# Sixteen of 22 channel tiles of the feed-forward's output half as seven products of quarters

## The chip, the cores and the metric

The kernel runs on one core of one Trainium2 chip. The metric is the device time of one execution in microseconds. Before the change it is 1206.3 us, the median of 3 runs (1205.36 to 1207.64).

## What is computed

Two layers of a hybrid encoder on 512 tokens of 1024 channels, in float32. Of each layer the change touches two parts, cut here to what matters:

```python
# attention: the indexer's scores choose the keys
score = sum over 4 index heads of relu(qi . ki) * wi        # 512 x 512, chunk-causal
keep the 128 highest of each row; softmax over the kept keys for 8 heads; times v
# feed-forward, D_FF = 2816 = 22 tiles of 128 channels
gate, up = split(x @ w_ffn_in)                              # 1024 -> 2 x 2816
ffn = (silu(gate) * up) @ w_ffn_out                         # 2816 -> 1024
x = layer_norm(ALPHA * x + ffn + ple)
```

## The kernel before

All matrix products are made of three matmuls each: both operands are split into a high part (a copy to float32r, on ScalarE) and a low part (the difference, on VectorE), and high x high, high x low and low x high are summed in PSUM. `split` (line 462) does this for a weight of up to 1024 columns: `A.copy(h, src)`, then `low(V, l, src, h)`. Its results go to a ring of four buffers for high parts (`wh`) and four for low parts (`wl`).

The feed-forward's input half is worked off by `ffn_in(j)` (line 1100), j = 0 to 10, 256 channels of gate and of up at a time. It uses seven products of quarters in place of eight. The sums of quarters of x are made once (`X1T.sums`), those of the weights per j: two by DMAs that add into a tile `tt` (`load_sums`, line 1085: two plain loads on SyncE's queue, then two accumulating ones on GpSimd's), two by VectorE. A product here is 24 matmuls of 256 columns into one PSUM bank. At the end the gated result is split into one tile `HT[j]` with 2 x 2 x 512 columns: high and low, two channel tiles, 512 tokens.

The output half is plain: `ffn_out(f0, f1, last)` (line 1168) multiplies channel tiles f0 to f1 of HT with `w_ffn_out`, for each of two column halves n and four token blocks b, three matmuls of 512 columns per channel tile. HT is the stationary operand, the split weight the moving one. Then VectorE adds each of the four banks to the rows X. The groups stand between the ffn_in:

```python
        for j in range(4):
            ffn_in(j)
        ffn_out(0, 6, False)
        for j in range(4, 7):
            ffn_in(j)
        ffn_out(6, 12, False)
        for j in range(7, 9):
            ffn_in(j)
        ffn_out(12, 16, False)
```

So one ffn_in lies between the last HT of a group and its ffn_out. After ffn_in(9) and ffn_in(10), `ffn_out(16, 22, True, ...)` ends the layer.

The order of the work is set by a planner in the file. Every engine call is recorded by `Recorder`, and `Order.issue` (line 160) sorts all calls into one list: each engine takes, among what its costs say can start within a small window, what the program has first. Buffers of a pool are given out in the order of the due times. Each engine then runs its own list strictly in order. As all calls are issued at one line, the profile's rows all say L276; they are told apart by the names of the tiles.

SBUF is divided by pools: `big` has 15 tiles of 2048 float32 per partition (x, HT, tt, quarters and much else), `page` 10 tiles of 512, five more pages `P` for scores and attention weights, three for masks, `raw` two tiles for weights as loaded. PSUM has four banks `acc`, three `ps`, one `po`.

Of the kernel before, what the change touches and what calls it, by code (L numbers as in the profile page):

```python
# [11 lines left out]
F32 = mybir.dt.float32  # L12
# [16 lines left out]
NB = 4  # L29
# [301 lines left out]
def body(ctx: ExitStack, tc: tile.TileContext, x, p, positions, w_in, w_o, ln1_g, ln1_b,  # L331
# [17 lines left out]
    def PP(dt, name):  # L349
        return page.tile([128, 512], dt, name=name, tag="P", bufs=5)  # L350

# [12 lines left out]
    def low(eng, dst, src, hi):  # L364
        eng.tensor_tensor(out=dst, in0=src, in1=f32(hi), op=OP.subtract)
# [113 lines left out]
    def wrows(w, r0, nkt, c0, c1):  # L479
        return w[r0:r0 + nkt * 128, c0:c1].rearrange("(k p) n -> p k n", p=128)  # L480
# [246 lines left out]
    for ly in range(DEPTH):  # L727
# [6 lines left out]
        wsc = small.tile([128, NB, 4], F32, name="wsc", bufs=2)  # L734
        sco = [None] * NB
# [363 lines left out]

        def ffn_in(j):  # L1100
# [52 lines left out]
            A.activation(g2, ba, AF.Silu)  # L1153
            ht = HT[j] = T(FR, "HT").rearrange("p (e f t) -> p e f t", e=2, f=2)
            for i, (g, u) in enumerate(((g1, s2), (g2, s5))):
                V.scalar_tensor_tensor(u, u, -1.0, g, op0=OP.mult, op1=OP.mult)
                v, ts = u.rearrange("p (f t) -> p f t", f=2), slice(i * 256, (i + 1) * 256)
                A.copy(ht[:, 0, :, ts], v)
                low(V, ht[:, 1, :, ts], v, ht[:, 0, :, ts])

# [25 lines left out]
        load_sums(0)  # L1186
        for j in range(4):
            ffn_in(j)
        ffn_out(0, 6, False)
        for j in range(4, 7):  # L1190
            ffn_in(j)
        ffn_out(6, 12, False)
        for j in range(7, 9):
            ffn_in(j)
        ffn_out(12, 16, False)
        for j in range(9, 11):
            ffn_in(j)
# [33 lines left out]
```

## Time and profile before

| | |
|---|---|
| median of 3 runs | 1206.3 us |
| profiled execution, its time | 1206.69 us |
| its span, first to last instruction | 1205.0 us |
| TensorE busy in the span | 1181.0 us |
| VectorE busy | 911.2 us |
| ScalarE busy | 594.1 us |
[...]

The span leaves out 1.7 us around the first and last instruction. Busy is the time in which at least one instruction of the engine ran. A recorded instruction is longer than the step from its start to the next start, for matmuls and on VectorE, as the next one starts before its end is written. The two layers take about 600 us each; the feed-forward of the first lies at 260 to 590 us.

### The profile page before, as it was taken

The numbers are of one execution on the slowest core, as the hardware profiler recorded it, in microseconds if no ns is written. First come the engines' busy times: TensorE is split into PE (matmuls) and PEld (weight loads), VectorE is DVE, ScalarE is ACT, GpSimd is POOL, SyncE is SP. The second block draws the span as 40 slices with busy tenths as digits, with TensorE's granted clock in tenths as the row PEclk, the third lists the DMA queues.
The fourth block names the chain that finished last, engine by engine and source line by source line (L and its number), as shares of the span: only waits on it lengthen the run. The fifth ranks groups of instructions, "written<-read, shape, count | busy, mean of one in ns | idle before, by whom it ended". The sixth has DMA issues, their size and how long they took to land. (4 is left out here: it accounts for less than half of the span.)

```text
span 1205.0 us, 18516 instructions
## 1 busy us (share of the span) xinstructions
PE 1181.0 (98%) x7326; PEld 1053.9 (87%) x7326; DVE 911.2 (76%) x1612; ACT 594.1 (49%) x978; POOL 154.4 (13%) x126
## 2 busy tenths in 40 slices
PE   8999999999999999999999999999999999999997
PEld 7877878789989998989888878778899899899995
DVE  6799998968755755757788999887777477566667
ACT  5545785545633533525345458934465245244340
POOL 0005312110100100000010261121010000000001
PEclk8999999999999999999999999999999999999999
DMA  7232143187871862743511321524685656648141
GB/s 219 71 98 78 36 88 140 36 192 206 183 199 60 188 198 70 208 108 98 192 53 36 121 73 36 140 70 159 150 197 144 173 125 173 175 106 209 53 141 70
DMA packets 124903, 152.76 MB, mean 127 GB/s; under 512 B 6544, under 2 KB 94608, under 8 KB 124816
## 3 DMA queue, kind: packets, MB, share of 16 engines
q1 hardware_dynamic: 101584, 128.51, 33.4%
q0 software_dynamic: 23232, 23.07, 12.5%
q8 instruction: 57, 0.93, 0.3%
q14 instruction: 30, 0.25, 0.1%
HBM read 149.47 MB, written 2.10 MB: 126 GB/s over the span
## 5 line engine op out<-in xcount | busy, mean ns | idle before, releaser
L276 DVE TENSOR_TENSOR wl<-raw,wh 128x1024 fp32r<-128x1024 f32 x178 | 217.3, 1223 | 126.6 <-ACT wh L276 125.7
L276 ACT CAST wh<-raw 128x1024 fp32r<-128x1024 f32 x194 | 203.4, 1050 | 211.1 <-PE acc L276 138.8
L276 PE MATMUL acc<-x1s,wh 128*128 128x256 f32 x1408 | 254.7, 283 | 2.3 <-ACT fg L276 2.3
L276 PEld LDWEIGHTS acc<-x1s,wh 128*128 128x128 f32 x1408 | 219.6, 192 | 2.7 <-ACT fg L276 2.7
L276 PE MATMUL acc<-wh,HT 128*128 128x512 f32 x704 | 218.5, 389 | 0.1
L276 PE MATMUL acc<-x1s,wl 128*128 128x256 f32 x704 | 199.2, 283 | 0.0
L276 PE MATMUL acc<-x1q,wh 128*128 128x256 f32 x1056 | 191.3, 283 | 0.0
L276 PEld LDWEIGHTS acc<-x1q,wh 128*128 128x128 f32 x1056 | 165.2, 192 | 0.6
L276 PEld LDWEIGHTS acc<-wh,HT 128*128 128x128 f32 x704 | 132.1, 188 | 27.6 <-issue 0.5
L276 PE MATMUL acc<-x1q,wl 128*128 128x256 f32 x528 | 149.4, 283 | 0.0
L276 DVE TENSOR_TENSOR wl<-tt,wh 128x1024 fp32r<-128x1024 f32 x66 | 80.8, 1224 | 76.3 <-ACT wh L276 76.2
L276 PE MATMUL acc<-wl,HT 128*128 128x512 f32 x352 | 137.1, 389 | 0.0
L276 PEld LDWEIGHTS acc<-x1s,wl 128*128 128x128 f32 x704 | 135.2, 192 | 0.0
L276 ACT CAST wh<-tt 128x1024 fp32r<-128x1024 f32 x66 | 69.3, 1050 | 130.4 <-PE acc L276 69.3
L276 POOL DMA_DIRECT2D tt<-in_w_ffn_in x44 | 56.4, 1303 | 527.8 <-DMA tt<-in_w_ffn_in 394.2
L276 PEld LDWEIGHTS acc<-x1q,wl 128*128 128x128 f32 x528 | 101.3, 192 | 0.0
L276 PE MATMUL acc<-wh,x1q 128*128 128x512 f32 x256 | 80.2, 392 | 1.4 <-DVE x1q L276 1.0
L276 PEld LDWEIGHTS acc<-wl,HT 128*128 128x128 f32 x352 | 66.1, 188 | 13.5
L276 PE MATMUL acc<-wl,xth 128*128 128x512 f32 x192 | 75.4, 395 | 1.5 <-DVE wl L276 1.5
L276 PE MATMUL acc<-wh,xtl 128*128 128x512 f32 x192 | 75.0, 393 | 0.0
L276 PE MATMUL acc<-wh,xth 128*128 128x512 f32 x192 | 74.9, 396 | 0.1
L276 ACT COPY fg<-acc 128x512 f32<-128x512 f32 x66 | 38.7, 586 | 65.0 <-PE acc L276 65.0
(214 smaller groups left out, 2024.6 us busy)
## 6 DMA issues: line engine op xcount, KB each, us to landing
raw<-in_w_ffn_in SPq DMA_DIRECT2D x22, 1024.0 KB, 5.3
tt<-in_w_ffn_in SPq DMA_DIRECT2D x44, 512.0 KB, 6.0
tt<-in_w_ffn_in POOLq DMA_DIRECT2D x44, 512.0 KB, 7.0
raw<-in_w_ffn_out SPq DMA_DIRECT2D x16, 1024.0 KB, 5.2
raw<-in_w_in SPq DMA_DIRECT2D x12, 1024.0 KB, 5.4
raw<-in_w_ffn_in SPq DMA_DIRECT2D x22, 512.0 KB, 3.6
raw<-in_w_ple_gate SPq DMA_DIRECT2D x8, 1024.0 KB, 5.1
raw<-in_w_ffn_out SPq DMA_DIRECT2D x12, 512.0 KB, 3.8
```

What stands on the lines that cost most here:

```text
L276: o.ins = o.fn(*o.a, **o.k)
```

## The change

In each layer the channel tiles 0 to 15 of the output half (j = 0 to 7) are multiplied by seven products of quarters as well, in groups of three, three and two j (six, six and four channel tiles). Tiles 16 to 21 stay as they were. HT of j below 8 takes two big tiles instead of one: `ha` holds the quarters h11, h12, h22, `hb` four sums of quarters (P1, S2, S3, S4), each split into high and low. Two of the seven weight operands, t1 and t3, are made by accumulating DMAs into two more big tiles per group (`load_out`, called inside the group's last ffn_in), two by VectorE. A product is, per j, two token blocks of three matmuls of 512 columns. After each product VectorE adds its two banks to X or takes them off.

To make room, the pools change: `big` 17 tiles, `page` 8. The scores and masks of a layer now share one big tile, and the attention weights P lie in a ring of four slots in another. The diff, cut:

```diff
-    big = ctx.enter_context(tc.tile_pool(name="big", bufs=15))
-    page = ctx.enter_context(tc.tile_pool(name="page", bufs=10))
+    big = ctx.enter_context(tc.tile_pool(name="big", bufs=17))
+    page = ctx.enter_context(tc.tile_pool(name="page", bufs=8))
...
-            sc = sco[b] = PP(F32, "sc")[:, :L]
+            if not scores:
+                scores.append(T(F32, "sc"))
+            sc = sco[b] = scores[0][:, (b - 1) * 512:(b - 1) * 512 + L]
...
-            m = mask[b] = page.tile([128, 512], BF, name="mask", tag="mask", bufs=3)[:, :(b + 1) * 128]
+            o = (0, 1536, 1664, 256)[b]
+            m = mask[b] = scores[0][:, o:o + (b + 1) * 64].bitcast(BF)
...
+            ring = T(F32, "P").rearrange("p (i n) -> p i n", i=4)
...
-                P = P_[b, h] = PP(F32, "P")[:, :L]
+                P = P_[b, h] = ring[:, (8 * b + h) % 4, :L]
...
+            if js:
+                out_sums.append(load_out(js))
             load_sums(j + 1)
...
+            ha, hb = HT[j] = [T(FR, "HT").rearrange("p (e q) -> p e q", e=2) for _ in range(2)]
...
+            parts(ha, 0, s2)
+            parts(ha, 512, h22)
+            ya, yb = page_(), page_()
+            p1, y2, y3, y4 = ya[:, 0:256], ya[:, 256:512], yb[:, 0:256], yb[:, 256:512]
+            V.tensor_tensor(out=p1, in0=h22, in1=h21, op=OP.subtract)
+            V.scalar_tensor_tensor(y2, p1, -1.0, h11, op0=OP.mult, op1=OP.subtract)
+            parts(hb, 0, ya)
+            V.tensor_tensor(out=y3, in0=h11, in1=h21, op=OP.subtract)
+            V.scalar_tensor_tensor(y4, y2, -1.0, h12, op0=OP.mult, op1=OP.subtract)
+            parts(hb, 512, yb)
...
+        def load_out(js):
...
+            for first in (q[0][0], q[1][1]):
+                t = T(F32, "tt")[:, :n * 512]
+                v = t.rearrange("p (j n) -> p j n", j=n)
+                SY.dma_start(v, first)
+                G.dma_start(v, q[0][1], accum_op=OP.add)
+                ts.append(t)
...
+        def ffn_seven(js, loaded):
...
+            def product(banks, src, which, first):
...
+                for j0 in range(0, n, 2):
+                    m = min(2, n - j0)
+                    hl.append(split(src[:, j0 * 512:(j0 + m) * 512].rearrange("p (j n) -> p j n", j=m),
+                                    [m, 512], V))
+                for i in range(2):
+                    for k, j in enumerate(js):
...
+                        for z, (a_, b_) in enumerate(((hs[0], wh), (hs[0], wl), (hs[1], wh))):
+                            PE.matmul(banks[i], a_, b_, start=first and k + z == 0,
+                                      stop=k == n - 1 and z == 2, skip_group_check=True)
...
+            product(ba, w11, A11, True)
+            into(ba, 0, 0, OP.add)
+            product(bb, w21, A12, True)
+            into(bb, 0, 0, OP.add)
+            bc = [PS() for _ in range(2)]
+            product(bc, t1, P1, True)
+            into(bc, 1, 1, OP.subtract)
+            w22 = fetch(q[1][1])
+            V.tensor_tensor(out=t1, in0=t1, in1=w22, op=OP.add)
+            product(ba, t1, S2, False)
+            into(ba, 0, 1, OP.subtract)
+            product(bc, w22, S4, False)
+            into(bc, 0, 1, OP.subtract)
+            product(ba, t3, S3, False)
+            into(ba, 1, 1, OP.subtract)
+            V.tensor_tensor(out=w21, in0=w21, in1=t1, op=OP.add)
+            product(ba, w21, A22, False)
+            into(ba, 1, 0, OP.add)
...
-        for j in range(4):
-            ffn_in(j)
-        ffn_out(0, 6, False)
...
+        for js in ([0, 1, 2], [3, 4, 5], [6, 7]):
+            for j in js:
+                ffn_in(j, js if j == js[-1] else None)
+            ffn_seven(js, out_sums.pop())
+        for j in range(8, 11):
+            ffn_in(j)
```

The change also moves instructions on the engines. In the lists below numbers at the names tell tiles of one name apart; X_76 and X_77 are the rows of x, acc and ps PSUM banks, wh and wl the split weights, fg pages of the gated result.

VectorE in the first layer, where the first group of the output half begins. Before (ffn_in(3) has just ended; HT_790 is its result, the group multiplies the three HT ahead of it):

```order
L276 SCALAR_TENSOR_TENSOR fg_775<-fg_775,fg_789 128x512
L276 TENSOR_TENSOR HT_790<-fg_778,HT_790 128x2x256
L276 TENSOR_TENSOR HT_790<-fg_775,HT_790 128x2x256
L276 TENSOR_TENSOR wl_805<-raw_803,wh_804 128x1024
L276 TENSOR_TENSOR wl_807<-raw_803,wh_806 128x1024
L276 TENSOR_TENSOR wl_814<-raw_812,wh_813 128x1024
L276 TENSOR_TENSOR X_76<-acc_796,X_76 128x512
L276 TENSOR_TENSOR X_76<-acc_797,X_76 128x512
L276 TENSOR_TENSOR X_77<-acc_798,X_77 128x512
L276 TENSOR_TENSOR X_77<-acc_799,X_77 128x512
```

The group's next splits stand ahead of the adds, and the newest HT is not used until the group after.

VectorE at the same place with the change (ffn_in(2) has just ended; fg_738 and fg_739 hold the sums of its result, HT_736 and HT_737 are its two tiles, tt_711 is t1, raw_745 is w21, raw_760 w22):

```order
L276 TENSOR_TENSOR wl_753<-raw_745,wh_752 128x512
L276 TENSOR_TENSOR wl_757<-tt_711,wh_756 128x1024
L276 TENSOR_TENSOR X_76<-acc_742,X_76 128x512
L276 TENSOR_TENSOR wl_759<-tt_711,wh_758 128x512
L276 TENSOR_TENSOR tt_711<-tt_711,raw_760 128x1536
L276 TENSOR_TENSOR X_76<-acc_743,X_76 128x512
L276 TENSOR_TENSOR raw_745<-raw_745,tt_711 128x1536
L276 TENSOR_TENSOR wl_762<-tt_711,wh_761 128x1024
L276 TENSOR_TENSOR wl_764<-tt_711,wh_763 128x512
L276 TENSOR_TENSOR wl_766<-raw_760,wh_765 128x1024
L276 TENSOR_TENSOR HT_737<-fg_738,HT_737 128x512
L276 TENSOR_TENSOR HT_737<-fg_739,HT_737 128x512
```

Where splits and four adds to X stood, there are now adds to X, splits and the two in-place sums of 1536 columns; the low parts of HT_737 come last, and both sums stand ahead of the low part wl_762. Ahead of this piece stand one gated half, two low parts of HT_736, the sums of quarters and two adds to X.

TensorE at the same place with the change, from the end of P1's matmuls for the first two j (HT_677 and HT_706; HT_737 belongs to the third):

```order
L276 MATMUL ps_755<-wl_757,HT_706 128x512
L276 MATMUL ps_755<-wh_756,HT_706 128x512
L276 MATMUL acc_740<-wh_761,HT_677 128x512
L276 MATMUL acc_741<-wh_761,HT_677 128x512
L276 MATMUL acc_740<-wl_762,HT_677 128x512
L276 MATMUL acc_740<-wh_761,HT_677 128x512
L276 MATMUL acc_740<-wh_761,HT_706 128x512
L276 MATMUL acc_740<-wl_762,HT_706 128x512
L276 MATMUL acc_740<-wh_761,HT_706 128x512
L276 MATMUL acc_741<-wl_762,HT_677 128x512
L276 MATMUL ps_754<-wh_758,HT_737 128x512
L276 MATMUL ps_754<-wl_759,HT_737 128x512
```

P1 is broken off after two of its three j, six matmuls of S2 on acc_740 and two on acc_741 are put in, and P1's matmuls for the third j follow. Before, the list runs the same HT through four banks in turn:

```order
L276 MATMUL acc_796<-wh_792,HT_712 128x512
L276 MATMUL acc_796<-wl_793,HT_712 128x512
L276 MATMUL acc_796<-wh_792,HT_712 128x512 x2
L276 MATMUL acc_796<-wl_793,HT_712 128x512
L276 MATMUL acc_796<-wh_792,HT_712 128x512
L276 MATMUL acc_797<-wh_792,HT_712 128x512
```

Up to the first group of the feed-forward's output half TensorE's list has the same instructions in the same order as before.

## Rows read from the trace of the kernel before

**Rows 1.** The page, part 1: busy us (share of span) x instructions.

```profile
PE 1181.0 (98%) x7326; PEld 1053.9 (87%) x7326; DVE 911.2 (76%) x1612; ACT 594.1 (49%) x978; POOL 154.4 (13%) x126
```

**Rows 2.** Busy time by 25 us stretch; columns in the first line.

```profile
core 0: us, PE busy (x) PEld busy (x) DVE busy (x) ACT busy (x) POOL busy (x), PEclk, DMA share, GB/s
75.00:100.00 25.00, 23.47 (x114) 19.36 (x113) 24.51 (x65) 10.63 (x16) 9.70 (x9) 1.00 0.37 127
100.00:125.00 25.00, 24.02 (x123) 19.77 (x122) 24.53 (x49) 13.01 (x23) 12.19 (x10) 1.00 0.16 50
300.00:325.00 25.00, 25.00 (x211) 25.00 (x210) 19.55 (x21) 13.79 (x18) 5.08 (x4) 1.00 0.73 177
350.00:375.00 25.00, 25.00 (x112) 20.70 (x111) 11.13 (x12) 4.62 (x5) 1.95 (x2) 1.00 0.47 105
```

**Rows 3.** Groups by line, VectorE and ScalarE, 250 to 590 us; page columns of part 5.

```profile
L276 DVE TENSOR_TENSOR wl<-raw,wh 128x1024 fp32r<-128x1024 f32 x65 | 79.5, 1223 | 57.6 <-ACT wh L276 57.5
L276 DVE TENSOR_TENSOR X<-acc,X 128x512 f32<-128x512 f32 x28 | 18.5, 686 | 7.2 <-PE acc L276 7.2
L276 DVE TENSOR_TENSOR HT<-fg,HT 128x512 fp32r<-128x512 f32 x22 | 14.6, 688 | 0.8
L276 DVE TENSOR_TENSOR tt<-tt,raw 128x1024 f32<-128x1024 f32 x11 | 13.5, 1225 | 0.9 <-DMA raw<-in_w_ffn_in 0.6
L276 DVE TENSOR_TENSOR wal<-raw,wah 128x256 fp32r<-128x256 f32 x2 | 0.9, 426 | 0.1
L276 ACT CAST wh<-raw 128x1024 fp32r<-128x1024 f32 x65 | 68.2, 1049 | 74.5 <-PE acc L276 60.5 <-DVE raw L276 8.6 <-issue 2.9
L276 ACT CAST HT<-fg 128x512 fp32r<-128x512 f32 x22 | 13.4, 619 | 1.8 <-DVE fg L276 1.8
```

**Rows 4.** Timeline of VectorE: start us, us, instruction, [idle before].

```profile
300.02 1.23 DVE L276 TENSOR_TENSOR tt<-tt,raw 128x1024 f32<-128x1024 f32 x1
301.16 0.68 DVE L276 TENSOR_TENSOR fg<-acc,fg 128x512 f32<-128x512 f32 x1
303.58 1.28 DVE L276 SCALAR_TENSOR_TENSOR fg<-fg 128x512 f32<-128x512 f32 x2
315.64 0.68 DVE L276 TENSOR_TENSOR fg<-acc,fg 128x512 f32<-128x512 f32 x1
316.24 1.22 DVE L276 TENSOR_TENSOR wl<-raw,wh 128x1024 fp32r<-128x1024 f32 x1
```

**Rows 5.** Timeline where the last ffn_in ahead of an ffn_out ends.

```profile
343.52 0.28 PE L276 MATMUL acc<-x1q,wl 128*128 128x256 f32 x1
343.64 0.40 PE L276 MATMUL acc<-wh,HT 128*128 128x512 f32 x1
343.84 0.60 ACT L276 ACTIVATE fg<-acc 128x512 f32<-128x512 f32 x1 [1.38 <-PE acc L276]
344.47 0.69 DVE L276 SCALAR_TENSOR_TENSOR fg<-fg 128x512 f32<-128x512 f32 x1 [0.68 <-ACT fg L276]
345.08 1.46 DVE L276 TENSOR_TENSOR HT<-fg,HT 128x512 fp32r<-128x512 f32 x2
```

**Rows 6.** Timeline of a wait of the matmuls for VectorE.

```profile
83.84 2.35 DVE L276 TENSOR_TENSOR wl<-raw,wh 128x1024 fp32r<-128x1024 f32 x2
85.11 0.50 PE L276 MATMUL acc<-wl,xth 128*128 128x512 f32 x1 [1.53 <-DVE wl L276]
85.45 0.40 PE L276 MATMUL acc<-wh,xtl 128*128 128x512 f32 x1
```

**Rows 7.** The page, part 6: DMA issues, KB each, us to landing.

```profile
tt<-in_w_ffn_in SPq DMA_DIRECT2D x44, 512.0 KB, 6.0
tt<-in_w_ffn_in POOLq DMA_DIRECT2D x44, 512.0 KB, 7.0
raw<-in_w_ffn_out SPq DMA_DIRECT2D x16, 1024.0 KB, 5.2
raw<-in_w_ffn_out SPq DMA_DIRECT2D x12, 512.0 KB, 3.8
```

More of the change, by code (lines that the diff above doesn't have):

```diff
@@ L347, in PG @@
         return page.tile([128, n], dt, name=name, tag="page")
-    def PP(dt, name):
-        return page.tile([128, 512], dt, name=name, tag="P", bufs=5)
     def ACC():
@@ L734, in body @@
         wsc = small.tile([128, NB, 4], F32, name="wsc", bufs=2)
-        sco = [None] * NB
+        sco, scores = [None] * NB, []
         mask = [mask0] + [None] * 3
@@ L1098, in load_sums, with ffn_in @@
                 G.dma_start(v[:, i], wrows(wf_l, 0, 4, DFF + c0, DFF + c0 + 256), accum_op=OP.add)
-        def ffn_in(j):
+        PLAIN = 8
+        out_sums = []
+        def ffn_in(j, js=None):
             c0 = j * 256
@@ L1153, in ffn_in @@
             A.activation(g2, ba, AF.Silu)
[L1154 to L1155 removed]
+            for u, g in ((s2, g1), (s5, g2)):
                 V.scalar_tensor_tensor(u, u, -1.0, g, op0=OP.mult, op1=OP.mult)
[L1157 to L1159 removed]
+            if j >= PLAIN:
+                ht = HT[j] = T(FR, "HT").rearrange("p (e f t) -> p e f t", e=2, f=2)
+                for i, u in enumerate((s2, s5)):
+                    v, ts = u.rearrange("p (f t) -> p f t", f=2), slice(i * 256, (i + 1) * 256)
+                    A.copy(ht[:, 0, :, ts], v)
+                    low(V, ht[:, 1, :, ts], v, ht[:, 0, :, ts])
+                return
@@ new lines, in ffn_in, with parts @@
+            ha, hb = HT[j] = [T(FR, "HT").rearrange("p (e q) -> p e q", e=2) for _ in range(2)]
+            def parts(t, q0, src):
+                q = slice(q0, q0 + src.free_size())
+                A.copy(t[:, 0, q], src)
+                low(V, t[:, 1, q], src, t[:, 0, q])
+            h11, h12, h21, h22 = s2[:, 0:256], s2[:, 256:512], s5[:, 0:256], s5[:, 256:512]
+            parts(ha, 0, s2)
+            parts(ha, 512, h22)
+            ya, yb = page_(), page_()
+            p1, y2, y3, y4 = ya[:, 0:256], ya[:, 256:512], yb[:, 0:256], yb[:, 256:512]
@@ new lines, in ffn_in @@
+            V.tensor_tensor(out=p1, in0=h22, in1=h21, op=OP.subtract)
[5 more added lines that the diff above has]
+        def load_out(js):
+            n = len(js)
+            w = wfo_l[js[0] * 256:(js[-1] + 1) * 256].rearrange("(j e p) n -> e p j n", e=2, p=128)
+            q = [[w[e][:, :, i * 512:(i + 1) * 512] for i in range(2)] for e in range(2)]
+            ts = []
+            for first in (q[0][0], q[1][1]):
[4 more added lines that the diff above has]
+                ts.append(t)
+            return q, ts
@@ new lines, in ffn_seven, with fetch, into @@
+        def ffn_seven(js, loaded):
+            n = len(js)
+            q, (t1, t3) = loaded
+            def fetch(src):
+                return raw(lambda t: [(t[:, :n * 512].rearrange("p (j n) -> p j n", j=n), src)])[:, :n * 512]
+            def product(banks, src, which, first):
+                hl = []
+                for j0 in range(0, n, 2):
[4 more added lines that the diff above has]
+                    for k, j in enumerate(js):
+                        wh, wl = (x[:, k % 2] for x in hl[k // 2])
+                        t = HT[j][which // 3 > 0]
+                        o = (which if which < 3 else which - 3) * 256 + i * 128
+                        hs = t[:, 0, o:o + 128], t[:, 1, o:o + 128]
+                        for z, (a_, b_) in enumerate(((hs[0], wh), (hs[0], wl), (hs[1], wh))):
+                            PE.matmul(banks[i], a_, b_, start=first and k + z == 0,
+                                      stop=k == n - 1 and z == 2, skip_group_check=True)
+            def into(banks, half, cols, op):
+                cs = slice(cols * 512, (cols + 1) * 512)
+                for i in range(2):
+                    x = Xb(2 * half + i)[:, cs]
+                    if op == OP.add:
+                        V.tensor_tensor(out=x, in0=banks[i], in1=x, op=op)
+                    else:
+                        V.tensor_tensor(out=x, in0=x, in1=banks[i], op=op)
+            A11, A12, A22, P1, S2, S3, S4 = range(7)
+            ba, bb = [ACC() for _ in range(2)], [ACC() for _ in range(2)]
+            w11, w21 = fetch(q[0][0]), fetch(q[1][0])
+            product(ba, w11, A11, True)
[16 more added lines that the diff above has]
+            into(ba, 1, 0, OP.add)
```

7 lines of the change are left out of this document (removed).

## The prediction

> **What bounds the kernel now.** The page's first part comes first: TensorE is busy for 1181.0 of 1205.0 us, VectorE for 911.2 [rows 1]. Busy times are averages, so the table of stretches comes next. In the feed-forward TensorE is busy for the whole 25 us of a stretch at a clock of 1.00, with an ffn_in (300 to 325) as with an ffn_out (350 to 375); VectorE has 19.55 and 11.13 us to do there [rows 2]. In attention (75 to 125) VectorE is nearly full with 24.5 us and TensorE idles for 1 to 1.5 us [rows 2]. So in the stage that is changed the time is TensorE's: a matmul that goes is worth its step, as long as the other engines hand over in time. They do so now; VectorE waits for casts there (57.6 us ahead of the weights' low parts) [rows 3].
>
> The step of a matmul is read from the counts, since records overlap. In the ffn_out stretch 112 matmuls of 512 columns fill 25 us: 0.223 us each. An ffn_in's are 211 in 25 us, 0.118 each [rows 2].
>
> **What goes from TensorE.** For channel tiles 0 to 15 the plain form takes 16 tiles x 4 token blocks x 2 column halves x 3 = 384 matmuls a layer. The new one takes 7 products x 8 j x 2 token blocks x 3 = 336, of the same shape and with the same operand held. 48 x 0.223 = 10.7 us a layer, **21.4 us** in two.
>
> **What VectorE and ScalarE get.** VectorE's step is shorter than a record: an addition of 1024 columns begins at 300.02, the next at 301.16, so 1.14 us; one of 512 takes 0.60 (315.64 to 316.24; the pair of 1.28 at 303.58 agrees) [rows 4]. The slope gives estimates of 0.33 for 256 columns (a record of 0.43 against 0.69 for 512 bears that out [rows 3]) and 1.68 for 1536.
>
> Per ffn_in with j below 8, HT's low parts grow from 2 to 3 of 512 and one of 256, and four sums of 256 are new: 0.60 + 5 x 0.33 = 2.3 us on VectorE. Per three-j group there are 7 splits of 1024 and 512, 14 adds to X and two sums: 7 x 1.74 + 14 x 0.60 + 2 x 1.68 = 23.9 us beside 126 x 0.223 = 28.1 us of matmuls. The two-j group has 7 x 1.14 + 14 x 0.60 + 2 x 1.14 = 18.7 beside 84 x 0.223 = 18.7: no room at all, but plain ffn_in follow. An ffn_in takes 168 x 0.118 = 19.9 us, of which VectorE is busy now for 19.9 / 25 x 19.55 = 15.6; 2.3 more still leave 2 us. So VectorE is not the bound in sum; what counts is the order in which it delivers. ScalarE stays far off: 13.79 of 25 in an ffn_in [rows 2], and in a three-j group 7 casts of 1024 and of 512 columns, 7 x (1.05 + 0.62) = 11.7 of 28.1 [rows 3]. Its added casts cost nothing as long as they run ahead of VectorE.
>
> **The new wait, a three-j group.** Big tiles held when the group starts are 2 of x, 3 quarters and 4 sums of x, five HT, t1, t3 and the sums for the next ffn_in: 17. The sixth HT (HT_737) must wait until t1 is done with, and P1 needs it. The list shows the consequence: P1 broken off, S2 put in.
>
> The clock starts where ffn_in ends. In the trace that is 343.64; ScalarE's gate begins 0.20 later, VectorE's product with it at 344.47, so at +0.83, and the first low part at 345.08 [rows 5]. From there VectorE works off in order: eight instructions of 512 columns, five of 256, wl_757 of 1024 and both sums, and only then wl_762: 8 x 0.60 + 5 x 0.33 + 1.14 + 2 x 1.68 = 10.95. No X add in between has to wait, as its matmuls end earlier. So wl_762 begins at 0.83 + 10.95 = 11.78, its record ends 1.22 later, and a matmul that waited for such a low part started 0.05 after its end (83.84 + 1.22 = 85.06; 85.11) [rows 6]: 13.05. TensorE has 36 matmuls of A11 and A12, 12 of P1 and 2 of S2 ahead: 50 x 0.223 = 11.16. It stands for 1.9 us, and the matmul after the wait takes 0.34 until the next (85.11 to 85.45), some 0.1 more than usual: **2.0 us**. HT_737's low part comes after wl_762, 0.60 and 1.14 more: 14.66 + 0.69 + 0.05 = 15.40. TensorE reaches it ten matmuls after its restart, at 13.05 + 0.1 + 2.23 = 15.39: no second stall. Afterwards the splits of S4, S3 and A22 come 1 to 3 us ahead.
>
> **The two-j group.** A tile is free for every HT here. VectorE has nine of 512 and five of 256 ahead of S2's low part: 0.83 + 5.40 + 1.65 = 7.88, with record and step 9.15; TensorE gets there after 39 matmuls, at 8.70: 0.56 with the slow first matmul. Ahead of A22 its sum and split stand behind the adds of S4 and S3 and come 0.3 late: 0.4. Together **1.0 us**.
>
> Two groups of three and one of two cost 5.0 us a layer, 10.0 in all. Bounds: 0 (both late low parts are covered by matmuls that I took as shorter than they are), and 3.6 us per group on six groups, which eats the gain.
>
> **At nothing, with cover.** Six more accumulating DMAs a layer on GpSimd's queue (busy 154.4 of 1205.0 us [rows 1]) and more loads: t1 and t3 are issued before the group's last ffn_in, with 20 us to land; a 512 KB load takes 6.0 and its accumulation 7.0, 1.5 times that is 20 for both [rows 7], and t1 is first cast some 4 us into the group. SyncE's queue holds the sums for the next ffn_in behind them, again a whole group ahead. w21 is loaded once the last ffn_in's fourth sum is split, some 8 us before the end; with 3.8 to 5.2 for 512 to 1024 KB [rows 7] it just makes it, and 1 us more would show in A12. In attention TensorE's list is the same; four slots of P are enough, as a slot is read two heads after it is written. The smaller page pool adds a few waits of ScalarE there, where VectorE is the bound: between 0 and 4 us, I take 0. The gaps don't cost the clock: it is granted at 1.00 in the stretch with the 1.53 us wait [rows 2, 6].
>
> [...] An addition that reads a PSUM bank steps at 0.60 us, like one that reads SBUF only [rows 4]. [...]
>
> **Sum.** 1206.69 is the profiled execution's own time (span 1205.0 and 1.7 around), 0.4 above the median of 1206.3. 1206.7 - 21.4 + 10.0 = **1195.3 us**.
>
> **Rivals.**
> 1. *Nothing is lost* (0.17): the late low parts are covered, since casts and hops are shorter in a busy queue than in my chain; then 1185.3, to 1190 with half a microsecond per group. For it: no stall of TensorE in the feed-forward now. Against it: wl_762 stands behind two sums.
> 2. *The split ring is exposed* (0.11, slower). Four wh and wl hold two products. The third's first buffer is free only near the end of the first; a cast of 1.05 and a low part of 1.22 [rows 3] follow, and in VectorE's queue two adds of 0.60 stand ahead: 3.5 us against the 4.0 of the second product. Where a sum or an add waiting for its bank comes in between as well, the product starts late. It decides from 0.5 us on each of the 42 products (21.4 / 42); at 0.8 us on each the time is 1206.7 - 21.4 + 33.6 = 1219. Against it: in most products the list has the splits ahead of those adds.
> 3. *The pools take it back* (0.12): scores' pages and P's ring hold up attention by 4 us a layer and the groups lose 10 to 14: 1203 to 1209.
>
> **Numbers.** My forecast, 1190 to 1203, has 0.60. A measurement of this kernel can tell some 0.2% (2.4 us) from no change: below 1203.9 lie the forecast, the first rival and a little of the third. So faster 0.79, same 0.10, slower 0.11. The range leaves out rival 2, the upper part of rival 3 and the very best of rival 1: 1186 to 1206.
>
> **What would show it.** Right: 96 matmuls fewer, TensorE busy for about 21 us less, a wait for wl of about 1.9 us in the third product of each three-j group, shorter ones in the two-j group, the same step of 0.223, attention unchanged. Rival 1: TensorE full at 25.00 throughout the groups. Rival 2: a wait ahead of nearly every product, for wh or wl. Rival 3: TensorE idle longer between 75 and 250 us. The forecast is wrong if the waits per group are under 0.5 or over 3.5 us, or if they name a DMA.

## The result and the profile after

| | before | after |
|---|---|---|
| median of the runs (range) | 1205.8 us (1203.7 to 1207.6) | 1212.8 us (1211.2 to 1213.0) |
| profiled execution, its time and span | 1206.69, 1205.0 us | 1212.49, 1210.8 us |
| mean granted clock of TensorE, as a share of full speed | 0.995 | 0.992 |

The change makes the kernel slower: ratio 1.0056, interval 1.0044 to 1.0069. The forecast was 1195.3 us, range 1186 to 1206. First the page after, parts 1, 3 (queue: packets, MB, share of 16 engines' span) and 6 (KB, us to landing):

```profile
PE 1168.0 (96%) x7230; PEld 1036.2 (86%) x7230; DVE 1007.4 (83%) x1794; ACT 633.1 (52%) x1048; POOL 169.4 (14%) x138
...
q1 hardware_dynamic: 103792, 132.70, 34.4%
q0 software_dynamic: 27520, 31.46, 16.1%
...
tt<-in_w_ffn_in POOLq DMA_DIRECT2D x44, 512.0 KB, 8.2
...
raw<-in_w_ffn_out SPq DMA_DIRECT2D x12, 768.0 KB, 8.7
...
tt<-in_w_ffn_out SPq DMA_DIRECT2D x8, 768.0 KB, 6.2
```

The 96 matmuls are gone (7326 to 7230 [rows 1]), yet TensorE's busy time fell by 13 us, not 21. And the loads of 768 KB in the three-j groups (w11, w21 and w22) take 8.7 us to land in the median, where 512 KB took 3.8 and 1024 KB 5.2 [rows 7]. In the second group w11 and w21 alone, from the view of DMAs over the issue of each:

```profile
raw<-in_w_ffn_out SPq DMA_DIRECT2D x1, 768.0 KB, 9.8
raw<-in_w_ffn_out SPq DMA_DIRECT2D x1, 768.0 KB, 8.9
```

Over the four three-j groups w11 takes 9.8 to 11.1 us and w21 8.3 to 9.0.

The timeline of TensorE after, instructions ahead of which it waited, the first layer's three groups and the start of the second layer's first (start us, us, instruction, [us waited and for whom]):

```profile
322.50 0.47 PE L276 MATMUL acc<-x1q,wh 128*128 128x256 f32 x2 [1.94 <-DVE fg L276]
329.15 0.50 PE L276 MATMUL acc<-wh,HT 128*128 128x512 f32 x1 [1.94 <-ACT HT L276]
340.90 0.50 PE L276 MATMUL acc<-wl,HT 128*128 128x512 f32 x1 [1.50 <-DVE wl L276]
416.40 0.47 PE L276 MATMUL acc<-x1q,wh 128*128 128x256 f32 x2 [0.32 <-DVE fg L276]
424.00 0.74 PE L276 MATMUL acc<-wh,HT 128*128 128x512 f32 x1 [2.87 <-ACT HT L276]
424.53 1.05 PE L276 MATMUL acc<-wl,HT 128*128 128x512 f32 x2
...
437.28 0.50 PE L276 MATMUL acc<-wl,HT 128*128 128x512 f32 x1 [1.51 <-DVE wl L276]
498.25 1.21 PE L276 MATMUL acc<-wh,HT 128*128 128x512 f32 x4 [0.26 <-DVE HT L276]
505.28 0.50 PE L276 MATMUL acc<-wl,HT 128*128 128x512 f32 x1 [0.56 <-DVE wl L276]
...
918.02 0.47 PE L276 MATMUL acc<-x1q,wh 128*128 128x256 f32 x2 [2.58 <-DVE fg L276]
```

The waits for wl are those of the forecast. So, in size, is the small one for HT in the two-j group, but not in place: the forecast had 0.4 ahead of A22, where the trace has no wait. Those for fg and for HT at the start of a three-j group are not in it. The second layer has two for fg (2.58 and 1.64), one for HT (0.95) and the same small ones. A wait costs about 0.3 us more than its record: that begins at the end of the matmul before, some 0.2 after its step, and the matmul behind the wait takes 0.33 until the next.

Where they come from is in the timelines of ScalarE and of VectorE after, around the first layer's second group:

```profile
413.34 1.57 ACT L276 CAST wh<-raw 128x1024 fp32r<-128x1024 f32 x2 [3.28 <-DMA raw<-in_w_ffn_out]
420.38 1.05 ACT L276 CAST wh<-raw 128x1024 fp32r<-128x1024 f32 x1 [5.47 <-DMA raw<-in_w_ffn_out]
421.34 0.63 ACT L276 ACTIVATE fg<-fg 128x512 f32<-128x512 f32 x1
421.87 0.58 ACT L276 ACTIVATE fg<-acc 128x512 f32<-128x512 f32 x1
423.32 0.62 ACT L276 CAST HT<-fg 128x512 fp32r<-128x512 f32 x1 [0.88 <-DVE fg L276]
```

```profile
414.43 1.23 DVE L276 TENSOR_TENSOR wl<-raw,wh 128x1024 fp32r<-128x1024 f32 x1 [2.50 <-ACT wh L276]
415.57 0.68 DVE L276 TENSOR_TENSOR fg<-acc,fg 128x512 f32<-128x512 f32 x1
...
421.46 1.23 DVE L276 TENSOR_TENSOR wl<-raw,wh 128x1024 fp32r<-128x1024 f32 x1 [4.01 <-ACT wh L276]
422.60 1.29 DVE L276 SCALAR_TENSOR_TENSOR fg<-fg 128x512 f32<-128x512 f32 x2
```

ScalarE stands for w11 and then 5.47 us for w21. Both gates and the cast of the last HT are behind that cast in its list, so the group's third j comes late: the wait named HT. VectorE stands for the low part of w11, and the add that empties a PSUM bank of ffn_in is behind it: the wait named fg. None of these waits of TensorE names a DMA, yet each begins at one.

The table of stretches after shows what the 16 DMA engines and the clock did (the column ahead of the last is the DMA share, the one ahead of that the clock):

```profile
core 0: us, PE busy (x) PEld busy (x) DVE busy (x) ACT busy (x) POOL busy (x), PEclk, DMA share, GB/s
400.00:405.00 5.00, 5.00 (x44) 5.00 (x43) 4.91 (x10) 4.33 (x8) 3.47 (x3) 1.00 1.13 257
405.00:410.00 5.00, 5.00 (x44) 5.00 (x43) 3.57 (x4) 3.04 (x5) 0.39 (x1) 1.00 1.11 238
410.00:415.00 5.00, 5.00 (x44) 5.00 (x43) 2.40 (x3) 1.63 (x3) 0.00 (x0) 1.00 1.20 234
415.00:420.00 5.00, 4.68 (x37) 4.42 (x36) 2.45 (x4) 0.00 (x0) 0.00 (x0) 1.00 1.11 308
420.00:425.00 5.00, 2.13 (x8) 1.39 (x8) 3.46 (x6) 3.51 (x6) 0.00 (x0) 0.91 0.19 73
425.00:430.00 5.00, 5.00 (x18) 3.88 (x17) 3.55 (x9) 1.57 (x2) 0.00 (x0) 0.75 0.00 0
```

From 400 to 420, the whole ffn_in, the DMA share is above 1. The recorded times of packets overlap, so the column goes over 1 (1.11 to 1.20 here); it shows a crowd and not by how much it is too large. The clock is below 1.00 after the gap of 2.87 us, and so in the second layer after that of 2.58 (0.90 and 0.76); after 1.94 twice within 7 us it stayed at 1.00. Behind the gap of 2.87 a matmul of 512 columns takes 0.43 instead of 0.23 (granted clock 0.50 from 424.5 to 427), behind that of 2.58 one of 256 columns 0.21 instead of 0.12 (0.50 from 919 to 922.2); matmul by matmul each costs 1.5 us.

**The sum, from the rows.** Waits that the forecast has, with the 0.26 counted for the 0.4: 1.50 or 1.51 four times, 0.56 and 0.58, 0.26 twice, 7.7 us, with 0.3 for each of eight 10.1 (forecast 10.0). Waits that it has not: fg 1.94 + 0.32 + 2.58 + 1.64, HT 1.94 + 2.87 + 0.95, together 12.2, with 0.3 for each of seven 14.3, and 3.0 for the clock: 17.3. The forecast of 1195.3 and this make 1212.6; measured 1212.49. (Two small terms cancel: the step of 512 columns is 0.228 instead of 0.227, 1 us over 672 matmuls, and a wait of 1.2 us at 860 has gone.)

### The profile page after: what moved, and what is told of

Read it like the earlier page. It is cut to its first block, busy times and chain, and to the rows that moved or that the text cites. A ratio compares the mean times of both kernels' runs of the same rounds, so it can differ in the third digit from the quotient of the medians.

```text
span 1210.8 us, 18681 instructions
## 1 busy us (share of the span) xinstructions
PE 1168.0 (96%) x7230; PEld 1036.2 (86%) x7230; DVE 1007.4 (83%) x1794; ACT 633.1 (52%) x1048; POOL 169.4 (14%) x138
## 3 DMA queue, kind: packets, MB, share of 16 engines
q1 hardware_dynamic: 103792, 132.70, 34.4%
q0 software_dynamic: 27520, 31.46, 16.1%
## 5 line engine op out<-in xcount | busy, mean ns | idle before, releaser
L276 ACT CAST wh<-raw 128x1024 fp32r<-128x1024 f32 (+1 forms) x202 | 203.8, 1016 | 191.8 <-PE acc L276 63.3
L276 DVE TENSOR_TENSOR wl<-raw,wh 128x1024 fp32r<-128x1024 f32 (+1 forms) x186 | 217.8, 1175 | 90.6 <-ACT wh L276 89.9
L276 PE MATMUL acc<-wh,HT 128*128 128x512 f32 x512 | 163.5, 395 | 6.4 <-ACT HT L276 5.8
L276 ACT CAST wh<-tt 128x1024 fp32r<-128x1024 f32 (+1 forms) x96 | 94.4, 996 | 136.1 <-DVE tt L276 84.9
L276 DVE TENSOR_TENSOR wl<-tt,wh 128x1024 fp32r<-128x1024 f32 (+1 forms) x96 | 110.2, 1155 | 36.1 <-ACT wh L276 36.0
L276 PEld LDWEIGHTS acc<-wh,HT 128*128 128x128 f32 x512 | 96.2, 189 | 30.1 <-ACT HT L276 7.8
L276 PE MATMUL acc<-wl,HT 128*128 128x512 f32 x256 | 100.8, 398 | 7.2 <-DVE wl L276 7.2
L276 PEld LDWEIGHTS acc<-wl,HT 128*128 128x128 f32 x256 | 48.5, 189 | 19.9 <-DVE wl L276 10.4
L276 PEld LDWEIGHTS acc<-wh,x1q 128*128 128x128 f32 x256 | 47.9, 188 | 12.4 <-DVE x1q L276 1.8
```

Source lines behind the costliest of these rows:

```text
L276: o.ins = o.fn(*o.a, **o.k)
```

## The experiments

All times stand beside runs of the kernel before on the same chip; ratios are to it.

### What makes the loads late

**e1** leaves out the accumulation into t1 and t3:

```diff
-                G.dma_start(v, q[0][1], accum_op=OP.add)
```

> Leaves out the accumulation into t1 and t3 of the output groups (two DMAs per group, so these operands are plain quarters of the weights). Theory A, the accumulating DMAs crowd out the loads of w11 and w21, and ScalarE and VectorE hold the gates behind those late weights: the 768 KB loads land in 4 to 5.5 us instead of 8.7, TensorE's waits for fg and HT (12.2 us in all) and the two falls of the clock go, the waits for wl of 1.5 us stay; 1193 to 1198 us. Theory B, the loads are late because the two raw buffers come free late, whatever else is on the link: the waits for fg and HT stay above 8 us; 1208 to 1213.

Measured 1197.8 us, ratio 0.9935 (0.9920 to 0.9949). The page of e1, part 6, and its timeline of TensorE in the second group:

```profile
raw<-in_w_ffn_out SPq DMA_DIRECT2D x12, 768.0 KB, 5.2
```

```profile
415.76 0.50 PE L276 MATMUL acc<-wh,HT 128*128 128x512 f32 x1 [0.32 <-ACT HT L276]
427.51 0.50 PE L276 MATMUL acc<-wl,HT 128*128 128x512 f32 x1 [1.51 <-DVE wl L276]
```

The waits for fg are gone, that of 2.87 is 0.32, and those of 1.5 for wl stay. So with the weights on time the forecast's sum holds within 2.5 us, and the waits for HT that are left (0.88, 0.32 and 0.43, each with 0.3) are 2.5. By the ratio e1 is 7.8 us faster than the kernel before, where the forecast has 11.4.

**e13** sends the same bytes on the same queue, without adding; **e14** leaves out the second of the two accumulations:

```diff
-                G.dma_start(v, q[0][1], accum_op=OP.add)
+                G.dma_start(v, q[0][1])                               # e13
+                if first is q[0][0]:                                  # e14
+                    G.dma_start(v, q[0][1], accum_op=OP.add)
```

> The changed kernel with the two accumulating transfers per group sent as plain loads from the same queue into the same tiles (t1 and t3 are then both w12 alone: the output differs). Theory A1 (it is the adding that crowds the loads of w11 and w21): they land in 5.2 us, the fg waits go, 1197 to 1200, as without them. Theory A2 (it is the bytes in that stretch, whatever is done with them): 768 KB take 7.5 us or more, the fg and HT waits stay, 1209 to 1214.

> The changed kernel without the accumulation into t3; t1 is made as it was (S3 is then computed with w22 alone, so the output differs). Theory A (each of the two transfers crowds the weights): about half of the loss stays, 768 KB loads land in 6 to 7.5 us, 1201 to 1208. Rival (only the last transfer in flight does it, as it is the one that overlaps w21): 1197 to 1200, waits for fg gone.

Measured 1199.0 us (0.9949, 0.9934 to 0.9964) and 1199.3 (0.9950, 0.9935 to 0.9965). The pages of e13 and of e14, parts 3 and 6:

```profile
q0 software_dynamic: 25472, 31.46, 14.5%
...
raw<-in_w_ffn_out SPq DMA_DIRECT2D x12, 768.0 KB, 5.6
```

```profile
q0 software_dynamic: 25376, 27.27, 14.6%
...
raw<-in_w_ffn_out SPq DMA_DIRECT2D x12, 768.0 KB, 5.5
```

A1 holds: the same 31.46 MB cost 1.2 us over e1 as plain loads, so it is the adding. Of e14's two theories the rival was nearer: without one accumulation nearly the whole loss is gone, not half. The transfers one by one, in the three-j groups of both layers (us from issue to landing; last column: when the last transfer on GpSimd's queue lands, counted from w21's issue):

| | w11 | w21 | GpSimd's last |
|---|---|---|---|
| after | 9.8 to 11.1 | 8.3 to 9.0 | 9.1 to 9.7 |
| e13 | 8.1 to 9.4 | 5.2 to 6.4 | 3.2 to 4.7 |
| e14 | 8.6 to 9.2 | 4.9 to 6.4 | 2.9 to 4.9 |
| e1 | 5.5 to 7.5 | 4.5 to 5.9 | 1.8 to 3.8 |

GpSimd's accumulations land one after the other. In the second group after, that of t1 lands at 407.1, that of t3 at 413.1 and the two for the next ffn_in at 416.3 and 420.7, while w21 is in flight from 411.4 to 420.3. In e14 the last lands at 410.9, 4.0 us after w21's issue. So w21 is slow where accumulations fly beside it to its end. w11 is slow in e13 and e14 too, but lands 0.9 to 2.2 us sooner than after, group by group, and of the waits for fg only one of 1.07 (e13) and one of 0.21 (e14) are left.

The price of an accumulation can be worked out from the shares of queue q0. The page of before has, in part 3:

```profile
q0 software_dynamic: 23232, 23.07, 12.5%
```

12.5% of 16 x 1205.0 us is 2410 us of engine time, 16.1% of 16 x 1210.8 is 3119: 59 us for each of the 12 new transfers, or 3.7 us of all 16 engines. In e13 (14.5% of 16 x 1197.4 = 2778) it is 31 us, or 1.9. By these shares adding costs about twice the transfer. They are sums of packet times, which overlap, and take the 44 older transfers as unchanged, so these are estimates.

### Can they go elsewhere in time

**e2** and **e3** issue t1 and t3 in the group's first ffn_in, or its last but one:

```diff
-                ffn_in(j, js if j == js[-1] else None)
+                ffn_in(j, js if j == js[0] else None)                 # e2; e3: js[-2]
```

> t1 and t3 are loaded and accumulated inside the first ffn_in of a group instead of the last; nothing else. Theory A: as without the accumulations, w11 and w21 land in 4 to 6 us, the waits for fg and HT fall below 3 us; 1194 to 1200. Theory B: 1210 to 1214, the same waits.

> t1 and t3 are loaded inside the last ffn_in but one of a group. Theory A: the accumulations end about 10 us before w11 is issued, so 1194 to 1200 as well. Theory B: 1210 to 1214.

Both miss: 1240.8 us (1.0294, 1.0277 to 1.0310) and 1250.0 (1.0370, 1.0352 to 1.0387). Timelines of ScalarE and TensorE in e2:

```profile
382.53 1.04 ACT L276 CAST wh<-raw 128x1024 fp32r<-128x1024 f32 x1 [9.99 <-DMA raw<-in_w_ffn_in]
```

```profile
385.58 0.77 PE L276 MATMUL acc<-x1q,wh 128*128 128x256 f32 x2 [6.75 <-DVE fg L276]
```

The group's own weights are in time there (4.7 us), but the next ffn_in's weights are not: the same crowd, met by another load (it was issued at 365.8 and landed at 382.4, 16.6 us), and at 385 to 390 the granted clock is 0.53.

**e6** moves the sums for the next ffn_in behind S2 instead, **e8** does so with groups of two j:

```diff
-            load_sums(j + 1)
+            if not js:
+                load_sums(j + 1)
...
             product(ba, t1, S2, False)
+            load_sums(js[-1] + 1)
```

> The change, but the sums for the ffn_in after a group are loaded once the group's S2 is done, not ahead of the group: two accumulations fewer on the link while w11 and w21 come, and 16 big tiles held at the group's start, so HT's last tile has a slot at once. Crowding: w11 and w21 land in 5 to 7 us, the waits for fg and HT fall from 12 us to under 5; P1 is no longer broken off, so the waits for wl fall from 1.5 to about 1; the new risk is that the next ffn_in waits for its sums, up to 3 us in each of six places. 1193 to 1208. If the link is not the cause, the waits for fg and HT stay near 12 us.

> As with the sums loaded after S2, and in four groups of two j: the loads are 512 KB, and a group has 18.7 us of VectorE's work beside 18.7 of matmuls. Crowding: 512 KB land in 3.5 to 5 us, waits for fg and HT under 3 us; but the next sums have only about 7 us from S2's split to their use, so each of 8 groups can wait 3 to 8 us for them: 1195 to 1240, and I expect slower than with three groups.

1224.3 us (1.0142, 1.0116 to 1.0169; a miss) and 1230.6 (1.0204, 1.0179 to 1.0229): 768 KB land in 5.0 us in e6, but now the ffn_in behind the groups waits (3.42 and 4.42 us ahead of products with sums of x in e6; 1.7 to 2.9 behind every group in e8). These waits do not begin at the sums, as the expectations have it, but at that ffn_in's own weights, which fly beside the sums: VectorE stands 3.20 and 4.24 us for a load of 512 KB that took 10.9 and 11.9 in e6, and ScalarE 1.7 to 3.7 for one of 1024 KB in e8 (7.0 us after the first group).

**e7** gives t1's transfers to a group's first ffn_in and t3's to its second, each behind the next sums. **e15** does this one ffn_in later in a layer's first group. **e16** is e7 with four groups of two j:

```diff
-            if js:
-                out_sums.append(load_out(js))
             load_sums(j + 1)
+            if js and j == js[0]:                                     # e15: js[-2 if j < 3 else 0]
+                out_sums.append(load_out(js))
+            if js and j == js[1]:                                     # e15: js[-1 if j < 3 else 1]
+                load_t3(out_sums[-1])
```

> t1 is loaded in a group's first ffn_in and t3 in its second, each behind the sums for the next ffn_in in the queues: one more accumulation per ffn_in instead of two in a burst. Crowding by bursts: no ffn_in waits for its sums as in the two kernels that loaded both early, w11 and w21 land in 4 to 6 us in the three-j groups, 1195 to 1203. If any accumulation more per ffn_in is too much for the link, waits for sums of 3 to 7 us appear as there, and the time is over 1215.

> The whole computation. The first group of a layer sends t1's transfers in its second ffn_in and t3's in its third, the other groups in their first and second, each behind the sums for the next ffn_in. Theory A: w11 and w21 meet t3's transfers at most in the first group; loads of 768 KB land in 6 us or less, the fg waits at the first group's start shrink to 1 us or less, and without the waits that the split in the first two ffn_in of the first group had (3.1 and 2.0 us at the start of the layers) the time is 1199 to 1206. Rival (the sums for the next ffn_in are pushed late in the same way wherever these transfers stand): waits for fg of 2 us and more inside the ffn_in, 1207 or more.

> The whole computation in four groups of two j, t1's transfers in a group's first ffn_in and t3's in its second, each behind the next sums. Transfers are 512 KB each. Theory A: as the two-j group of the changed kernel waits 0.26 and 0.57 us only, four of them lose some 1.1 us each, 8.8 in two layers, with the last product list whole (a tile is free for every HT): 1206.7 - 21.4 + 8.8 = 1194, up to 1204 where the denser transfers delay the sums. Rival (VectorE has 18.7 us for 18.7 us of matmuls in such a group and a full ffn_in behind it): the debt runs into the next ffn_in, waits for fg or wh of 2 us and more there, 1210 or more.

1210.0 us (1.0037, 1.0023 to 1.0050), 1205.3 (0.9997, 0.9988 to 1.0007) and 1207.8 (1.0021, 1.0008 to 1.0033). Spreading helps, down to no difference from before. Only e15 lies in the range of its theory A; e7 and e16 lie between their two. Beside the waits for wl, what is left is in a layer's first ffn_in (3.12 us for fg in e7 and 2.52 in e16, where before it is 1.10) or its second (1.92 and 2.80 for fg in e15).

**e4** changes only what the planner believes: it counts 8 us for w11, w21 and w22.

```diff
+                if id(o.out.tensor) in self.late:
+                    fin[o.i] = max(fin[o.i], at + 8000)
...
+                order.late[id(t.tensor)] = t
```

> Loads as they are, but the planner counts 8 us for the loads of w11, w21 and w22, so that it puts the gates and HT ahead of the cast of w21. Theory A: w11 and w21 still land after 8 to 9 us, but TensorE's wait for HT goes (from 5.8 us to under 1) and that for fg shrinks; 1200 to 1206. Theory B expects the same here. If the order of ScalarE is not what holds HT, the waits stay and the time is 1210 to 1214.

1213.3 us (1.0072, 1.0055 to 1.0089), where theory A had 1200 to 1206. The gates now stand ahead of w21's cast and the waits for HT at the group's start are gone, but those for fg stay (1.96 and 2.41 at the largest) and the two-j group's wait for wl grew to 3.09. Another order does not make a late operand early.

### Can another engine add

**e10** loads t1 and t3 plainly with w11 and w12, and GpSimd adds; **e11** also puts the sum for A22 behind S2's low parts; **e12** is e11 with VectorE adding:

```diff
-            for first in (q[0][0], q[1][1]):
+            for first in (q[0][0], q[0][1]):
...
-                G.dma_start(v, q[0][1], accum_op=OP.add)
+            G.tensor_tensor(out=ts[0], in0=ts[0], in1=ts[1], op=OP.add)
...
+            G.tensor_tensor(out=t3, in0=t3, in1=w22, op=OP.add)
             product(bc, w22, S4, False)
```

> The changed kernel without accumulating DMAs in the output half: t1 and t3 are loaded plainly with w11 and w12, and GpSimd adds (t1 + t3 during the last ffn_in of the group, t3 + w22 inside the group). The computation is whole again; the traffic is that of the run that left the accumulation out. Theory A: loads of 768 KB land in about 5.2 us, the fg waits and the falls of the clock go, the time is that of that run, 1197.8, plus 0 to 4 us: 1197 to 1202. Rival B (the late weights come from VectorE's and ScalarE's own load in the group): fg and HT waits of 1.5 us and more stay, 1208 or more. Rival C (GpSimd's sums, about 4.3 us for 1536 columns by its 1.42 us for 512, come late or hold VectorE up): waits at P1 or S3, above 1204.

> Both edits of the two runs before together. Theory A: the two losses are separate, so the gains add: the time of the run with GpSimd's sums less about 6 us, 1191 to 1196. Rival B (once one wait goes, HT_737, next in VectorE's list, is late by as much): the wait changes its name from wl to HT and the time stays within 2 us of the run with GpSimd's sums.

> As the run before, with VectorE adding in place of GpSimd: 2 x 1.68 us more per three-j group, 2 x 1.14 per two-j group, half of it in the ffn_in before. VectorE's sum becomes 23.9 + 1.7 = 25.6 of 28.1 us in the three-j group. Theory A: it still fits where the sums stand behind S2's low parts; 1192 to 1199. Rival: VectorE becomes the bound inside the groups, waits for wl or HT of 1 us and more in each of six groups: 1200 to 1206.

1239.1 us (1.0281, 1.0261 to 1.0301), 1241.1 (1.0305, 1.0289 to 1.0320) and 1222.7 (1.0141, 1.0124 to 1.0158): all miss theory A, and e12 its rival's range too. The weights land in 5.0 us in e10. GpSimd and VectorE in e10, second group, from their timelines:

```profile
425.94 3.71 POOL L276 TENSOR_TENSOR tt<-tt,raw 128x1536 f32<-128x1536 f32 x1 [17.73 <-DMA raw<-in_w_ffn_out]
```

```profile
426.19 0.68 DVE L276 TENSOR_TENSOR X<-acc,X 128x512 f32<-128x512 f32 x1
428.20 1.73 DVE L276 TENSOR_TENSOR HT<-fg,HT 128x256 fp32r<-128x256 f32 x1 [1.33 <-ACT HT L276]
```

A low part of 256 columns takes 1.73 us instead of 0.42 and ends 0.3 us after GpSimd's sum; the addition that reads PSUM takes its usual 0.68 in the middle of it. So in e10 GpSimd's sum held VectorE up: rival C. In the two-j groups S2 then waits 5.08 us for its cast: VectorE's sum for it begins only at 512.01, behind a low part of 1024 columns that took 3.42 us instead of 1.22 beside GpSimd's sum, and behind adds to X; how much of the 5.08 each of these makes is not shown. Of the 41 us over e1, TensorE's waits in the feed-forward are 23 (33.6 for 10.7), and a mean granted clock of 0.984 for 0.998 makes some 17, as an estimate over 1237 us. In e11 the rival held: the sixth HT comes 1.2 to 1.6 us late, and the time is 2.0 us from e10's. In e12 VectorE does both sums ahead of the sixth HT, which comes 3.2 us late in each three-j group.

### The waits that were forecast

**e9** moves one sum in VectorE's list, that for A22, behind S2's low parts:

```diff
+            split_done = max(o.i for o in order.ops if o.engine == "DVE")
...
             V.tensor_tensor(out=w21, in0=w21, in1=t1, op=OP.add)
+            order.ops[-1].after.append(split_done)
```

> The changed kernel with one instruction moved on VectorE: the sum for the last product (w21 and t1) stands behind the low parts of S2 in its list and no longer ahead of wl_762. Theory A (two separate losses: the accumulating DMAs make w11 and w21 late, about 12 us of waits named fg and HT; and S2's low part stands behind two in-place sums, four waits of 1.5 us): the four waits of 1.5 us for wl shrink to 0.3 or less, the fg and HT waits stay; 1212.7 - 6 = 1206 to 1208. Rival B (the low part of S2 waits for its cast on ScalarE anyway): the waits for wl stay above 1 us and the time stays at 1211 to 1214.

1216.6 us (1.0098, 1.0083 to 1.0113). Timeline of TensorE in e9, second group:

```profile
434.07 0.50 PE L276 MATMUL acc<-wl,HT 128*128 128x512 f32 x1 [0.53 <-DVE wl L276]
438.19 0.50 PE L276 MATMUL ps<-wh,HT 128*128 128x512 f32 x1 [1.55 <-ACT HT L276]
```

The wait for wl fell from 1.51 to 0.53, and the sixth HT, now behind the sum, came 1.55 late. With 0.3 for the second gap that is 0.9 us more in each of four groups, 3.5; measured 3.8, or 5.1 by the ratios. Neither theory had this: S2's low part and the sixth HT come one right after the other, as in the prediction's chain (the HT there at 15.40, TensorE at it at 15.39), so what is put behind the one delays the other.

**e17** keeps t1's accumulation and lets VectorE add w22 to t3, behind the low parts of the sixth HT. **e18** further orders VectorE's list: first sum, S2's low parts, second sum, sixth HT, S4's low parts.

```diff
-            for first in (q[0][0], q[1][1]):
+            for first in (q[0][0], q[0][1]):
...
-                G.dma_start(v, q[0][1], accum_op=OP.add)
+                if first is q[0][0]:
+                    G.dma_start(v, q[0][1], accum_op=OP.add)
...
+            ht_done = max(o.i for o in order.ops if o.engine == "DVE")
...
             product(bc, w22, S4, False)
+            V.tensor_tensor(out=t3, in0=t3, in1=w22, op=OP.add)
+            order.ops[-1].after.append(ht_done)
```

> The whole computation. t1 is made as in the changed kernel; t3 is loaded plainly with w12, and VectorE adds w22 in the group, behind the low parts of the sixth HT: 1.68 us in a three-j group, whose VectorE sum becomes 25.6 of 28.1 us, 1.14 in the two-j group. Theory A (the second accumulating transfer is the loss): weights land in 5.5 us as in the run that left it out, waits for wl of 1.5 us and one for HT remain, 1199.3 plus 0 to 3: 1199 to 1202.5. Rival (VectorE has no room for the sum): new waits for wl or HT of 1 us and more ahead of S3 and A22 in each group, or an ffn_in that starts late, 1204 or more.

> As the run before, with VectorE's list changed inside the group: the first sum, S2's two low parts, the second sum, the sixth HT's two low parts, and only then the low parts of S4. Theory A: S2's low part comes 1.68 us earlier and the HT follows without the 1.7 us of S4's low parts between (those cost 1.55 us of wait for HT in e9): waits per three-j group fall from 1.5 to 0.5 for wl and 0 to 0.3 for HT; 1 us less in each of four groups, 4 in all: 1195 to 1199. Rival (S4 or S3 is late instead, since its low parts now stand behind HT and the adds to X): a wait of 1 us and more for wl at S4, no gain over the run before.

e17 takes 1203.1 us (0.9978, 0.9968 to 0.9988): the whole computation, 0.2% faster than the kernel before and 0.8% under the changed one (0.9978 / 1.0056). The time lies between theory A (to 1202.5) and the rival (from 1204). Its page and its timeline of TensorE, second and third group:

```profile
PE 1167.2 (97%) x7230; PEld 1032.5 (86%) x7230; DVE 1016.3 (85%) x1800; ACT 633.1 (53%) x1048; POOL 161.9 (13%) x132
...
raw<-in_w_ffn_out SPq DMA_DIRECT2D x12, 768.0 KB, 5.4
```

```profile
416.88 0.50 PE L276 MATMUL acc<-wh,HT 128*128 128x512 f32 x1 [0.41 <-ACT HT L276]
428.63 0.50 PE L276 MATMUL acc<-wl,HT 128*128 128x512 f32 x1 [1.51 <-DVE wl L276]
...
502.81 0.50 PE L276 MATMUL acc<-wl,HT 128*128 128x512 f32 x1 [0.43 <-DVE wl L276]
505.70 0.97 PE L276 MATMUL acc<-wh,HT 128*128 128x512 f32 x2 [0.31 <-ACT wh L276]
```

It is what e14 has, and in the two-j group, where the prediction found no room on VectorE, two short waits that e14 has not: e14 is 3.8 us faster without the sum. e18 is slower again, 1209.8 us (1.0035, 1.0024 to 1.0046). Its timeline of TensorE in the second group:

```profile
428.46 0.50 PE L276 MATMUL acc<-wl,HT 128*128 128x512 f32 x1 [0.53 <-DVE wl L276]
431.43 0.50 PE L276 MATMUL ps<-wh,HT 128*128 128x512 f32 x1 [0.42 <-ACT HT L276]
439.68 0.73 PE L276 MATMUL acc<-wh,HT 128*128 128x512 f32 x2 [0.81 <-ACT wh L276]
440.94 0.50 PE L276 MATMUL acc<-wl,HT 128*128 128x512 f32 x1 [0.53 <-DVE wl L276]
```

wl and HT came down together (0.53 and 0.42 for 1.51), but the splits that were pushed back are late 11 us on: 2.29 in four waits for 1.51 in one, with 0.3 each 1.7 us more per group, 6.8 in four; measured 6.7. The rival held in kind: no wait is as long as the 1 us that it had, but there are two, for wh and wl.

### The pools

**e5** is the kernel before with the new pools alone: 17 big tiles, 8 pages, scores and masks in one tile, P in a ring of four.

```diff
-    big = ctx.enter_context(tc.tile_pool(name="big", bufs=15))
-    page = ctx.enter_context(tc.tile_pool(name="page", bufs=10))
+    big = ctx.enter_context(tc.tile_pool(name="big", bufs=17))
+    page = ctx.enter_context(tc.tile_pool(name="page", bufs=8))
```

> The kernel before with the change's SBUF alone: 17 big tiles, 8 pages, scores and masks in one tile, P in a ring of four; the feed-forward as before. My reading: attention is not touched, 1203 to 1208, no difference from before. Rival: the pools are what costs, 1209 to 1215.

1205.5 us beside 1206.0, ratio 0.9999 (0.9990 to 1.0009): they cost nothing.

## Why the prediction was wrong

- *What bounds the kernel, and what goes from TensorE.* Right: 96 matmuls of 0.227 us each, 21.8 us. (The prediction's 0.223 counts 112 records in 25 us, some of which reach over the edges of the stretch.) With the weights on time e1 is 8 us faster than before.
- *The new wait of the three-j group.* Right in place and cause, 1.5 and 0.3 us for a forecast of 2.0 (restart within it); the two-j group's 1.4 for 1.0, one of its two waits in another place. In all 10.1 for 10.0, which is closer than the parts are: there chance helped. e9 shows also that wl_762 and HT_737 are bound to each other as in the prediction's chain.
- ***At nothing, with cover*: the step that failed.** "w21 ... with 3.8 to 5.2 for 512 to 1024 KB [rows 7] it just makes it, and 1 us more would show in A12." It landed in 8.3 to 9.0, and w11, of which the prediction says nothing, in 9.8 to 11.1. The landing times were taken from rows without the new transfers beside them [rows 7], and the factor of 1.5 was given to t1 and t3 alone, not to what flies with them. The work of the DMA engines could have been added up. By the page after, q1 moves 132.70 MB in 34.4% of 16 x 1210.8 us, 50 us of engine time or 3.14 us of all 16 per MB. An ffn_in has 2.6 MB of plain loads, 8.2 us, and two accumulations (2410 / 44 = 55 us of engine time, 3.4 of all 16): 15 of its 20 us, as the share of 0.73 had it [rows 2]. Into the last one come t1 and t3, 1.57 MB and two accumulations at 3.7, and w11 and w21, 1.57 MB: 12.3 and 4.9 us. As an estimate, 32 us of work meet 20 us. But the sum is a warning and no verdict: done in the same way it is 25 us for e1 and some 29 for e13 and e14, all over 20, and of the 15 us that the changed kernel loses to e1 those two lose 1.5 at most. What tells those from the changed kernel is the last column of the table above: how long accumulations still land when w21 is under way.
- *Where a late w21 shows.* Not in A12, as the prediction has it, but earlier: its cast stands ahead of both gates and of an HT in ScalarE's list, and w11's low part ahead of a bank's release in VectorE's. Of the 17.3 us, 6.5 are waits for fg and 5.8 for HT. The prediction's own sign of being wrong, waits of over 3.5 us per group, is there in all four three-j groups: 5.4, 4.7, 4.1 and 4.1.
- *"The gaps don't cost the clock."* In this run true of gaps to 1.94 us, as of that of 1.53 [rows 6]; after 2.58 and 2.87 the granted clock was 0.50 for some 3 us each, which cost 3.0 us in all. Longer gaps were not in the forecast, so this follows from the failed step; e1, without them, has a mean of 0.998 for 0.992. But the length of a gap does not settle it: behind the wait of 3.09 in e4 a matmul of 512 columns takes 0.43 (495.8 to 501.4), behind that of 3.12 in e7 one of 256 still takes 0.12 (268.8 to 274), and e6 has 0.43 again (437.3 to 439.8) behind waits of 0.15, 0.73 and 0.63.
- *Rival 1, nothing is lost:* no, the four waits for wl stayed in e1, e13 and e14. *Rival 2, the split ring:* its time (1219) was no nearer than 6 us, its mechanism absent, as no wait stands ahead of most products. *Rival 3, the pools:* fell with e5. The case that came, late weights, was named in the text as a margin and had no rival and no chance of its own.
- *Additions that read a PSUM bank.* Right: they step at 0.60 us after as well (430.74 to 431.34), as in the rows [rows 4].

Open: whether it must be the second accumulation. The table shows why one more can carry nearly the whole loss (with it the accumulations last until w21 has landed), but leaving out the first one instead was not tried.

## What to carry to other kernels

Where a change adds transfers, add up what all of them cost the 16 DMA engines in the stretch they share, accumulating ones at twice a plain load (3.7 for 1.9 us of all 16 here, by estimate), and look, queue by queue, at what is still landing when the load that matters is issued; a landing time from a row without the new transfers is no bound (3.8 to 5.2 us there, 8.3 to 9.0 with them). Then look in the in-order lists for what stands behind the first operand that may come late, as the wait can carry that name and not the transfer's (here fg and HT). Between operands that are late one after the other on one engine, reordering moved a wait and added a restart of 0.3 us (e9, e18).

## What was not expected of the hardware

- By the shares of their queue, accumulating transfers took about twice the packet time of plain ones of the same size (estimates of 3.7 and 1.9 us of all 16 engines for 768 KB in most of them), and two per group slowed loads of another queue from 5.6 to 8.7 us in the median.
- Two accumulations per group cost 15 us over none (1212.8 and 1197.8), one 1.5 (1199.3): far from a slope.
- In e10 GpSimd's sum of 1536 columns (3.71 us) held a VectorE instruction on SBUF for 1.3 us, and not one that read PSUM; one of 1024 columns (2.51 us) held another for 2.2 us.
